# Block-diagonal gate products: one matmul of 512 tokens and one of 8 samples in place of two halves of 260

## The chip, the cores and the metric

The kernel runs on one core of a Trainium2 chip. The metric is the device time of one launch in microseconds; the median of three runs before the change is 1004.61 us (1003.96 to 1005.44). The core's engines are TensorE (PE in the profile, its weight loads PEld), VectorE (DVE), ScalarE (ACT), GpSimd (POOL) and SyncE (SP, which issues most transfers). Each has its own queue of instructions, in the order that the program gives it.

## The reference, cut to what matters

The kernel computes one inference step of a hybrid decoder layer for 512 prompt tokens and 8 samples of one token each, so 520 columns (tokens) of width 1024. The layer has two branches, a matrix recurrence (HGRN2, eight heads) and a vector recurrence (RG-LRU, eight blocks of 128 channels), then a merge, an output projection and an MLP. The change is in the RG-LRU gates:

```
def _blockdiag(x, w):
    B, L, _ = x.shape
    xb = x.reshape(B, L, LRU_BLOCKS, LRU_BS)
    return jnp.einsum('blnd,nde->blne', xb, w.astype(F32)).reshape(B, L, LRU_WIDTH)

xc, buf = _causal_conv(xb, st_conv[l], lru_conv_w[l], lru_conv_b[l])
r = jax.nn.sigmoid(_blockdiag(xc, lru_wa[l]) + lru_ba[l].astype(F32))
ig = jax.nn.sigmoid(_blockdiag(xc, lru_wx[l]) + lru_bx[l].astype(F32))
hseq, h_last = _rglru(xc, r, ig, lru_lambda[l], st_lru[l].astype(F32))
```

For each of the eight blocks there are two products of a 128 x 128 weight with 128 x 520 activations, each followed by a bias and a sigmoid.

## The kernel before

Channels lie on the 128 partitions and the 520 tokens along the free dimension. Every f32 operand of a large product is split into a high and a low part in the type f32r, and a product is three matmuls: high x high, high x low and low x high. The profile shows f32r as f32 in matmul rows.

The program has four parts: a start (loads, conditioning, first norm), the recurrences (eight heads in four pairs, with two RG-LRU blocks per pair), the gates, branch projections and output projection, and the MLP. During the recurrences the main stream on TensorE are the input projections (`gemm`, line 120): eight steps over the contraction, each three matmuls for each of two halves of 260 tokens. They write to `mm`, two tiles of two PSUM banks. Around them stand the heads' products: transposes (lines 592, 695, 737), the blocks of 32 (line 629), and the 128 x 128 products (lines 705, 718, 720).

An RG-LRU block n begins in `rg_x`: its two weights are loaded and split (line 765), its input comes from a projection, the convolution runs on VectorE and the result `xc` is split into `xcs` (line 185). Its gates are made one projection later, by `rg_gates`, called from `gemm`: `blockdiag` for r (weight `lru_wa`) and for the input gate (`lru_wx`). Before the change `blockdiag` takes the 520 tokens in two halves of 260. For each half it asks for a tile `pb`, multiplies three times (line 780) and takes the sigmoid on ScalarE (line 159) into a tile `gate` of 520 columns. Later the gates feed the scan (`rg_scans`).

PSUM has eight banks: `mm` four, `ppt` one (tile `pt`), `ppb` one (tile `pb`), and `pps` two (tile `ps`). `pps` is the small pool: the heads' blocks of 32 (line 629), the transposes of the values (lines 561 and 592) and the conditioning products use it in turn. A tile that is asked for while the banks are taken waits for the last reader of an earlier one.

The order on each engine is set by a scheduler that places instructions as their operands become ready in its own simulation of time; `behind` adds an order between two instructions without a wait, and `urgent` raises the priority of some. An instruction whose result is not ready holds up all that stand behind it on its engine.

Of the kernel before, what the change touches and what calls it, by code (L numbers as in the profile page):

```python
# [6 lines left out]
F32 = mybir.dt.float32  # L7
# [9 lines left out]
L = 512  # L17
NB = 8
T = L + NB
HALF = T // 2  # L20
# [31 lines left out]
class Kernel:  # L52
# [716 lines left out]
            r.append((hi, lo))  # L769
        return r  # L770

    def blockdiag(self, w, x, bias):
        nc = self.nc
        o = self.slot(self.hg, "gate")
        (wh, wl), (xh, xl) = w, x
        for s in range(2):
            c = slice(s * HALF, (s + 1) * HALF)
            ps = self.ppb.tile([128, 512], F32, name="pb")
            for n, (a, b) in enumerate(((wh, xh), (wh, xl), (wl, xh))):
                self.behind(nc.tensor.matmul(ps[:, :HALF], a, b[:, c], start=n == 0, stop=n == 2), self.last_product)  # L780
            self.sigmoid(o[:, c], ps[:, :HALF], bias=bias)
        return o

    def rg_x(self, n):
# [20 lines left out]
    def rg_gates(self):  # L805
        if self.rg_pending is None:
            return
        (n, w, xs, xc), self.rg_pending = self.rg_pending, None
        r = self.blockdiag(w[0], xs, self.ba[:, n:n + 1])
        g = self.blockdiag(w[1], xs, self.bx[:, n:n + 1])  # L810
        self.nc.vector.tensor_tensor(g, g, xc, OP.mult)
        self.rg[n] = r, g

# [965 lines left out]
```

## Time and profile before

| | |
|---|---|
| median of three runs | 1004.61 us |
| the profiled execution | 1004.8 us |
| its span from first to last instruction | 1003.0 us |
| TensorE busy | 981.2 us, 9585 matmuls |
| weight loads busy | 954.5 us, 9585 loads |
| VectorE busy | 694.2 us |
| ScalarE busy | 513.4 us |
| gate matmuls (line 780) | 96, first at 77.6 us, last at 370.9 us |
| gate sigmoids (`gate<-pb`) | 32, 479 ns each |

In a row of a group, the shape behind a matmul is active rows * active columns of the weight and then the moving operand; the numbers behind the bar are the busy time of the group in us, the mean duration of one in ns, and the idle time of its engine just ahead of it. Matmuls are pipelined, so their durations overlap; the distance from one start to the next, the step, is seen in a timeline, where rows of equal instructions are merged (start, length, count). A windows row shows the busy time of each engine in a stretch.

### The profile page before, as it was taken

To read this page: it belongs to the slowest core of one execution; us is meant where nothing else is said; L and a number is where in the kernel's file an instruction comes from. 1 tells how busy PE (TensorE), PEld (TensorE's weight loads), DVE (VectorE), ACT (ScalarE), POOL (GpSimd) and SP (SyncE) were. 2 spreads that over 40 slices of the span, in tenths; PEclk is the share of its full clock that TensorE was granted. 3 is DMA by queue.
4 is the path that set the end of the run, shared out by engine and by line. 5 is a ranking of instruction groups with operands and counts; after the bars stand their busy time and mean duration, and the time that the engine had idled before them with its cause. 6 is when DMAs were issued, how large, how long until landed. Compare 5 with 4: busy or idle time off the path is not lost.

```text
span 1003.0 us, 23261 instructions
## 1 busy us (share of the span) xinstructions
PE 981.2 (98%) x9585; PEld 954.5 (95%) x9585; DVE 694.2 (69%) x1546; ACT 513.4 (51%) x987; POOL 112.4 (11%) x194
## 2 busy tenths in 40 slices
PE   6999999999999999999999999999999999999996
PEld 4799999999999999999989999999999999999996
DVE  6789698697878867563332347767766776777686
ACT  5444844664584456351222234466556645646664
POOL 3000000000000000120000000012321331232151
PEclk9999999999999999999999999999999999999998
DMA  9885435344434434686567765222762483274242
GB/s 299 239 257 146 133 102 155 95 146 137 117 105 133 127 98 126 208 272 193 167 190 228 231 183 157 85 85 53 168 160 71 102 194 99 54 174 91 63 85 86
DMA packets 212572, 145.78 MB, mean 145 GB/s; under 512 B 6262, under 2 KB 196878, under 8 KB 212458
## 3 DMA queue, kind: packets, MB, share of 16 engines
q1 hardware_dynamic: 202562, 132.37, 44.5%
q0 software_dynamic: 9904, 11.92, 6.4%
q8 instruction: 75, 1.23, 0.5%
q14 instruction: 31, 0.25, 0.1%
HBM read 123.61 MB, written 13.39 MB: 137 GB/s over the span
## 4 chain that ended last, share of the span: by engine, by line
PE 93%; ACT 2%; SPq 2%; DVE 1%; DMA 1%; issue 1%; DVEq 0%; ACTq 0%
PE mm L120 67%; PE ps L1152 8%; PE pt L1152 4%; PE pb L1152 2%; PE ps L629 2%; PE ps L385 1%; PE pb L780 1%; DMA w<-in_w_in_dram 1%; SPq L374 1%; PE pt L705 1%; SPq L74 1%; PE pt L718 1%; PE pt L629 1%; PE pt L720 1%; PE ps L395 0%
## 5 line engine op out<-in xcount | busy, mean ns | idle before, releaser
L120 PE MATMUL mm<-h,whi 128*128 128x260 f32 x3040 | 502.8, 285 | 2.9 <-ACT h L481 1.9
L120 PEld LDWEIGHTS mm<-h,whi 128*128 128x128 f32 x3040 | 421.5, 189 | 8.4 <-ACT h L481 2.6
L120 PE MATMUL mm<-h,wlo 128*128 128x260 f32 x1520 | 310.8, 284 | 0.0
L85 ACT CAST whi<-wst 128x1024 fp32r<-128x1024 f32 x165 | 172.6, 1048 | 217.6 <-PE mm L120 178.7
L88 DVE TENSOR_TENSOR wlo<-wst,whi 128x1024 fp32r<-128x1024 f32 x165 | 201.2, 1220 | 89.6 <-ACT whi L85 88.2
L120 PEld LDWEIGHTS mm<-h,wlo 128*128 128x128 f32 x1520 | 237.0, 189 | 0.0
L120 PE MATMUL mm<-a,whi 128*128 128x260 f32 x512 | 82.8, 283 | 0.0
L120 PEld LDWEIGHTS mm<-a,whi 128*128 128x128 f32 x512 | 70.3, 188 | 0.9 <-issue 0.8
L120 PE MATMUL mm<-a,wlo 128*128 128x260 f32 x256 | 51.7, 284 | 0.0
L881 POOL DMA_DIRECT2D t<-oaT_d x8 | 4.3, 549 | 383.9 <-DMA oaT_d<-e 377.1
L1248 DVE TENSOR_TENSOR f<-f 128x260 f32<-128x260 f32 x64 | 27.3, 427 | 28.9 <-ACT f L1243 28.2
L1240 POOL TENSOR_TENSOR ft<-ft,fsh 128x8 f32<-128x8 f32 x28 | 18.4, 658 | 215.8 <-DVE ft L1234 215.8
L1237 ACT ACTIVATE ft<-ft,fsh 128x512 f32<-128x512 f32 (+2 forms) x36 | 24.1, 676 | 36.0 <-DVE ft L1234 36.0
L120 PE MATMUL mm<-b,whi 128*128 128x260 f32 x256 | 41.6, 284 | 0.0
L120 PEld LDWEIGHTS mm<-a,wlo 128*128 128x128 f32 x256 | 39.4, 188 | 0.0
L120 PEld LDWEIGHTS mm<-b,whi 128*128 128x128 f32 x256 | 35.0, 188 | 2.5 <-issue 2.5
L615 DVE TENSOR_TENSOR Y<-Y,tb 128x512 f32<-128x512 f32 x40 | 27.5, 687 | 9.1 <-PE ps L629 6.0
L1285 POOL DMA_DIRECT2D ma<-snap x28 | 26.8, 959 | 40.0 <-issue 22.1
L897 DVE TENSOR_TENSOR t<-mm,t 128x520 f32<-128x520 f32 x8 | 5.6, 699 | 37.0 <-PE mm L120 37.0
L1264 POOL DMA_DIRECT2D ma<-snap x28 | 26.6, 948 | 38.2 <-DMA ma<-snap 22.5
L1243 ACT ACTIVATE f<-ft 128x520 f32<-128x520 f32 (+1 forms) x36 | 20.7, 586 | 14.9 <-POOL ft L1241 12.9
L120 PE MATMUL mm<-b,wlo 128*128 128x260 f32 x128 | 25.8, 283 | 0.0
(489 smaller groups left out, 1839.2 us busy)
## 6 DMA issues: line engine op xcount, KB each, us to landing
wst<-in_w_in_dram SPq DMA_DIRECT2D x63, 512.0 KB
wm<-in_w_mod_dram SPq DMA_DIRECT2D x8, 2048.0 KB
wst<-in_w_ff_dram SPq DMA_DIRECT2D x32, 512.0 KB
wst<-in_w_ff_dram SPq DMA_DIRECT2D x64, 256.0 KB
wm<-in_w_mod_dram SPq DMA_DIRECT2D x8, 1024.0 KB
st<-in_state_hgrn_dram SPq DMA_DIRECT2D x8, 512.0 KB
vb<-vd SPq DMA_DIRECT2D x8, 512.0 KB
out_dram<-st SPq DMA_DIRECT2D x8, 512.0 KB
```

Source lines behind the costliest of these rows:

```text
L85: ins = self.nc.scalar.copy(hi, st)
L88: ins = self.nc.vector.tensor_tensor(lo, st, hi.bitcast(F32), OP.subtract)
L120: self.last_product = self.nc.tensor.matmul(out[:, :c.stop - c.start], x, y[:, c], start=first and n == 0, stop=last and n == 2)
L615: made = nc.vector.tensor_tensor(view(Y, b, 0, 2 * b, n, b), view(X, b, 0, 2 * b, n, b), fac, OP.mult)
L629: ins = nc.tensor.matmul(*args, start=True, stop=True)
L1152: ins = self.nc.tensor.matmul(ps, x[:, w], y[:, f], start=j in (1, 7, 2) and k == 0 and n == 0, stop=k == 3 and n == 2, skip_group_check=True)
L1237: nc.scalar.activation(t[:, :p], t[:, :p], AF.Relu, bias=sh[:, 0:1])
L1240: eng.tensor_tensor(t[:, p:], t[:, p:], sh[:, 1:9], OP.add)
L1243: nc.scalar.activation(f, self.two(self.ft)[:, a:a + n], AF.Square)
L1248: self.nc.vector.tensor_tensor(f[:, n], f[:, a], f[:, b], op)
L1264: nc.gpsimd.dma_start(x[1][:, b], v[:, :n], accum_op=OP.add)
L1285: nc.gpsimd.dma_start(x[t][:, a], s[p], accum_op=OP.add)
```

## The change

`blockdiag` no longer halves the tokens. It takes one tile `pb` for the 512 prompt tokens and a slice of 8 columns, `few`, for the samples. For each of the three products it issues one matmul of 512 columns into `pb` and one of 8 columns into `few`, both with the same weight. Two sigmoids follow, of 512 and of 8 columns. `rg_gates` asks for both `few` tiles in the small pool `pps` ahead of the two calls. The count of matmuls (96) and of sigmoids (32) is the same.

```
-    def blockdiag(self, w, x, bias):
-        nc = self.nc
+    def blockdiag(self, w, x, bias, few):
         o = self.slot(self.hg, "gate")
         (wh, wl), (xh, xl) = w, x
-        for s in range(2):
-            c = slice(s * HALF, (s + 1) * HALF)
-            ps = self.ppb.tile([128, 512], F32, name="pb")
-            for n, (a, b) in enumerate(((wh, xh), (wh, xl), (wl, xh))):
-                self.behind(nc.tensor.matmul(ps[:, :HALF], a, b[:, c], start=n == 0, stop=n == 2), self.last_product)
-            self.sigmoid(o[:, c], ps[:, :HALF], bias=bias)
+        ps = self.ppb.tile([128, 512], F32, name="pb")
+        for n, (a, b) in enumerate(((wh, xh), (wh, xl), (wl, xh))):
+            for out, c in ((ps, slice(0, L)), (few, slice(L, T))):
+                self.behind(self.nc.tensor.matmul(out, a, b[:, c], start=n == 0, stop=n == 2, skip_group_check=True), self.last_product)
+        self.sigmoid(o[:, :L], ps, bias=bias)
+        self.sigmoid(o[:, L:], few, bias=bias)
         return o
...
-        r = self.blockdiag(w[0], xs, self.ba[:, n:n + 1])
-        g = self.blockdiag(w[1], xs, self.bx[:, n:n + 1])
+        few = [self.pps.tile([128, 512], F32, name="ps")[:, :NB] for _ in range(2)]
+        r = self.blockdiag(w[0], xs, self.ba[:, n:n + 1], few[0])
+        g = self.blockdiag(w[1], xs, self.bx[:, n:n + 1], few[1])
```

The scheduler also places the work anew. The order changes on TensorE, ScalarE, VectorE and SyncE during the recurrences; on TensorE it is the same again behind the recurrences, and GpSimd's order does not change. Two places on TensorE show what moves.

The first is in the second pair of heads, block 2, where the gate matmuls stand among the projections (`mm<-h`) and the transposes of the keys (`pt<-ident,X`). The names `bdh` and `bdl` are the high and low part of a gate weight, `wa` of r and `wx` of the input gate. Before, from the second r matmul of the first half on:

```order
L120 MATMUL mm<-h,wlo 128x260 x2
L695 MATMUL pt<-ident,X 128x128 x3
L780 MATMUL pb<-xcs,bdhlru_wa 128x260
L780 MATMUL pb<-xcs,bdllru_wa 128x260
L695 MATMUL pt<-ident,X 128x128
L120 MATMUL mm<-h,whi 128x260 x4
```

The same place now:

```order
L120 MATMUL mm<-h,wlo 128x260
L695 MATMUL pt<-ident,X 128x128 x2
L778 MATMUL pb<-xcs,bdhlru_wa 128x512
L778 MATMUL ps<-xcs,bdhlru_wa 128x8
L778 MATMUL pb<-xcs,bdllru_wa 128x512
L778 MATMUL ps<-xcs,bdllru_wa 128x8
L695 MATMUL pt<-ident,X 128x128 x2
L120 MATMUL mm<-h,wlo 128x260
```

The r gate is done in one group of matmuls here, each of 512 columns followed by one of 8 with the same weight; the second half's group, some 25 matmuls later before, is gone.

The second place is block 3 of the same pair, on TensorE again. Before, at its first r matmuls (`pt<-g,X` is the end of a head's output product):

```order
L720 MATMUL pt<-g,X 128x128
L780 MATMUL pb<-xcs,bdhlru_wa 128x260
L120 MATMUL mm<-h,whi 128x260
L780 MATMUL pb<-xcs,bdhlru_wa 128x260
L780 MATMUL pb<-xcs,bdllru_wa 128x260
L120 MATMUL mm<-h,whi 128x260 x3
```

Now:

```order
L778 MATMUL ps<-xcs,bdhlru_wa 128x8
L778 MATMUL ps<-xcs,bdhlru_wx 128x8
L120 MATMUL mm<-h,whi 128x260 x2
L120 MATMUL mm<-h,wlo 128x260 x2
L120 MATMUL mm<-h,whi 128x260
L778 MATMUL pb<-xcs,bdhlru_wa 128x512 x2
L778 MATMUL ps<-xcs,bdhlru_wa 128x8
L778 MATMUL pb<-xcs,bdllru_wa 128x512
L778 MATMUL ps<-xcs,bdllru_wa 128x8
L778 MATMUL ps<-xcs,bdhlru_wx 128x8
L778 MATMUL ps<-xcs,bdllru_wx 128x8
L120 MATMUL mm<-h,whi 128x260 x3
```

The 8-column matmuls of both gates are taken ahead of or together with r's large ones, up to three in a row, since both `few` tiles are there from the start; the block's first gate matmul now stands ahead of the head's output products instead of behind them.

## The prediction

> **What bounds the kernel now.** I read the page's shares first, then the chain of waits, then TensorE in windows by stage.
>
> ```profile
> span 1003.0 us, 23261 instructions
> PE 981.2 (98%) x9585; PEld 954.5 (95%) x9585; DVE 694.2 (69%) x1546; ACT 513.4 (51%) x987; POOL 112.4 (11%) x194
> PE 93%; ACT 2%; SPq 2%; DVE 1%; DMA 1%; issue 1%; DVEq 0%; ACTq 0%
> ```
>
> TensorE is busy for 98% of the span and holds 93% of the chain that ended last. A share is a mean, so the stage with the gates decides. They run in four bursts, one per pair of heads. The windows by stage:
>
> ```profile
> core 0: us, PE busy (x) PEld busy (x) DVE busy (x) ACT busy (x) POOL busy (x), PEclk, DMA share, GB/s
> 58.00:100.00 42.00, 42.00 (x533) 41.62 (x532) 38.17 (x105) 20.78 (x49) 0.00 (x0) 1.00 0.69 199
> 100.00:140.00 40.00, 39.36 (x509) 38.78 (x508) 31.03 (x89) 26.57 (x50) 0.00 (x0) 1.00 0.42 125
> 140.00:260.00 120.00, 120.00 (x1548) 118.86 (x1548) 97.39 (x266) 66.06 (x149) 0.00 (x0) 1.00 0.45 129
> 260.00:385.00 125.00, 125.00 (x1591) 123.85 (x1590) 98.10 (x266) 73.97 (x160) 0.00 (x0) 1.00 0.40 116
> 385.00:680.00 295.00, 295.00 (x2450) 282.09 (x2450) 153.41 (x282) 111.34 (x170) 17.33 (x34) 1.00 0.58 177
> 680.00:990.00 310.00, 309.70 (x2556) 309.43 (x2555) 224.84 (x371) 181.21 (x345) 83.54 (x136) 1.00 0.45 106
> PE pt L705 <- ACT g L698: 0.6, 1, 0.6
> ```
>
> The last row is the whole list of TensorE's waits from 58 to 680 us: one, of 0.6 us. So from 58 us to 990 us TensorE is full at full clock, whatever it gains or loses in the gate stage reaches the end one for one, and a saving on any other engine buys at most that 0.6 us. The question is what a pair "512 columns and 8 columns" costs TensorE against a pair of 260s.
>
> **What is removed.** All gate products before, by line and shape:
>
> ```profile
> L780 PE MATMUL pb<-xcs,bdhlru_wa 128*128 128x260 f32 x32 | 8.7, 314 | 0.0
> L780 PE MATMUL pb<-xcs,bdhlru_wx 128*128 128x260 f32 x32 | 6.8, 293 | 0.0
> L780 PE MATMUL pb<-xcs,bdllru_wa 128*128 128x260 f32 x16 | 4.5, 283 | 0.0
> L780 PE MATMUL pb<-xcs,bdllru_wx 128*128 128x260 f32 x16 | 4.5, 282 | 0.0
> L780 PEld LDWEIGHTS pb<-xcs,bdhlru_wa 128*128 128x128 f32 x32 | 5.5, 189 | 0.2
> ```
>
> That is 96 matmuls, each with its own weight load even where the same weight follows twice. The duration (283 ns) is latency, not price, as matmuls overlap; the price is the step from start to start. From TensorE's timeline, with one group of three:
>
> ```profile
> 87.28 0.41 PE L780 MATMUL pb<-xcs,bdhlru_wa 128*128 128x260 f32 x2
> 87.52 0.28 PE L780 MATMUL pb<-xcs,bdllru_wa 128*128 128x260 f32 x1
> 87.64 0.28 PE L120 MATMUL mm<-h,wlo 128*128 128x260 f32 x1
> ```
>
> Three steps in 87.64 - 87.28 = 0.36 us, 120 ns each. Removed: 96 x 0.120 = 11.5 us; a pair costs 240 ns.
>
> **What is added: 48 matmuls of 512 columns.** The trace has none in this type (f32r, which its rows show as f32). Nearest rows:
>
> ```profile
> L629 PE MATMUL ps<-Y 128*32 128x32 f32 x1152 | 15.2, 198 | 0.0
> L629 PE MATMUL pt<-st,fkq 128*32 128x128 f32 x128 | 5.6, 276 | 0.0
> L385 PE MATMUL ps<-wm,cT 128*32 128x512 f32 x128 | 15.4, 598 | 0.0
> L120 PE MATMUL mm<-h,whi 128*128 128x260 f32 x2528 | 470.8, 285 | 2.9 <-ACT h L481 1.9 <-DVE h L484 0.9
> L120 PE MATMUL mm<-h,whi 128*128 128x270 f32 x512 | 136.4, 287 | 0.0
> ```
>
> The first three are plain f32: (598 - 276) / 384 = 0.84 ns per column on a fixed 276 - 128 x 0.84 = 169 ns. With that fixed part an f32r matmul takes (284 - 169) / 260 = 0.44 ns per column, so 512 columns step 120 + 252 x 0.44 = 231 ns. Bounds: if the whole 120 ns scales, 512 / 260 x 120 = 236; if only the 2 to 3 ns between the 260 and 270 rows count (0.3 per column), 196. I take 231: its slope stands on rows hundreds of columns apart, the lower bound on ten.
>
> **48 matmuls of 8 columns.** Their streaming is nothing (8 x 0.44 = 4 ns), but each brings a full 128 x 128 weight load. Nearest is the pair on line 750, 64 columns behind a full weight. The weight loads there, then the matmuls:
>
> ```profile
> 417.99 0.31 PEld L750 LDWEIGHTS ps<-sq,ones_r 128*128 128x128 f32 x2
> 418.21 0.19 PEld L120 LDWEIGHTS mm<-h,wlo 128*128 128x128 f32 x1
> 418.32 0.55 PEld L120 LDWEIGHTS mm<-h,whi 128*128 128x128 f32 x4
> 417.98 0.28 PE L120 MATMUL mm<-h,wlo 128*128 128x260 f32 x1
> 418.10 0.33 PE L750 MATMUL ps<-sq,ones_r 128*128 128x64 f32 x2
> ```
>
> 64 columns stream in 64 x 0.84 = 54 ns, yet the four loads start 417.99, two steps later 418.21, then 418.32: 110 ns apart. With little to stream, the load sets the step. The load behind an 8-column matmul can hide under only 4 ns of streaming, so that matmul costs 110 ns. The loader runs one matmul ahead: line 750's first load starts at 417.99, just when the matmul before it starts (417.98), and not under the one before that. Bounds: above, 120 (the step of a full 260); below, 7 to 13 ns (15.2 us / 1152 for the 32 x 32 blocks, which load 32 columns and overlap on separate quarters of the array). I take 110, because the width of the weight is that of line 750 and not of the blocks.
>
> The Trainium skill, page "TensorE: Matmul & The Clock Gate", section "Back-to-back issue gap", gives a matmul of 1 to 64 columns about 60 cycles (25 ns) and one of N columns N / 2.4 + 2.5 ns, as the isolated gap without a weight-load budget. By it a pair would go from 2 x 111 to 216 + 25 ns and the change would cost 48 x 19 ns = 0.9 us, an estimate from that page. The 110 ns of the 64-column pair above speak against its 25 ns here; the mechanism that would give it, a load already there, is the first rival, priced from rows.
>
> **Sum.** 48 x (231 + 110 - 240) ns = 48 x 101 = +4.8 us. With both lower ends 48 x (196 + 7 - 240) = -1.8; with both upper ends 48 x (236 + 120 - 240) = +5.6; with 196 and 110, +3.2. The order of the new program puts up to three 8-column matmuls behind each other; that changes nothing, each exposes one load.
>
> **ScalarE and the banks.** Rows for the sigmoids, and the longest part of the gates' own wait:
>
> ```profile
> L159 ACT ACTIVATE gate<-pb,pa 128x260 f32<-128x260 f32 x32 | 15.3, 479 | 16.1 <-PE pb L780 16.0
> L159 ACT ACTIVATE X<-mm 128x520 f32<-128x520 f32 x16 | 9.6, 600 | 0.0
> L1169 ACT ACTIVATE snap<-ps 128x8 f32<-128x8 f32 x14 | 2.4, 169 | 0.0
> ```
>
> A gate goes from 2 x 479 = 958 ns to about 600 + 169 = 769 ns: 16 x 0.19 = 3 us less on ScalarE, which waits 16 us for these very matmuls; worth 0. The cover of this zero is TensorE's full queue; without it 3 us would be the most.
>
> The bank of `pb` now has two users per block instead of four. Between them stand 24 to 27 projection matmuls, 3 us, against under 1 us for the sigmoid plus its queue. Both banks of `ps` go to the samples. The tight place is the second one, whose first 8-column matmul comes after the blocks of 32 of line 629, once their last reader is done. ScalarE and TensorE there, before the change:
>
> ```profile
> 166.31 1.16 PE L629 MATMUL ps<-Y 128*32 128x32 f32 x80
> 170.84 0.51 ACT L679 COPY at<-ps 32x128 f32<-32x128 f32 x2
> 171.37 0.48 ACT L159 ACTIVATE gate<-pb,pa 128x260 f32<-128x260 f32 x1
> ```
>
> The reader ends at 171.35, 3.9 us after 167.47. In the new order 51 matmuls stand between, some 6 us by 120 ns, so 2 us are left. Cost 0; between 0 and 1 us is kept for the range, like the 0.6 us above. If a matmul does wait there, all projection products behind it in TensorE's queue wait, and with them the casts of the next weights.
>
> The profiled execution took 1004.8 us (span 1003.0), 0.2 above the median of the runs, 1004.61. So 1004.8 + 4.8 = 1009.6, and 1009.4 for the median.
>
> **Rivals.** *A second load ahead.* In the 231 ns of a 512 there is time for two loads of 110. If the loader uses it, an 8-column matmul costs its 4 ns and the 5 ns by which 120 exceeds 260 x 0.44: the pair is 231 + 9 = 240, no change, 1004.6; with the 196 for the 512 even 1003, the other side. It decides at the first load behind an 8-column matmul: started under the 512 or not. Against it: line 750. The same skill page, section "What happens when you issue a matmul", says loads are pulled ahead into a background weight buffer, without saying how many; the loads quoted at 418 us show one.
>
> *The small banks.* The samples hold both `ps` banks, and a matmul waits for a reader of line 679 or a sigmoid that stands late in ScalarE's queue. It takes over when that reader comes 6 us after line 629; the casts of weights that stand in that queue take 1.05 us each, and three more of them ahead of the reader in each of four bursts would make 3.9 + 3.2 = 7.1 us, 1 us too late: +4.8 + 4 x 1, 1013.4. For it: the reader already lags 3.9 us. The casts:
>
> ```profile
> L85 ACT CAST whi<-wst 128x1024 fp32r<-128x1024 f32 x165 | 172.6, 1048 | 217.6 <-PE mm L120 178.7
> ```
>
>  Against it are the 2 us left.
>
> *Two passes.* Plain f32 products are recorded twice:
>
> ```profile
> L705 PE MATMUL pt<-g 128*128 128x128 f32 x64 | 8.5, 276 | 0.6 <-ACT g L698 0.6
> ```
>
> 64 records for 8 heads x 4. If so narrow an f32r product is run like that, 48 loads more: +5.3, 1014.7. Against: all f32r rows (line 780: 96 of 96) are single.
>
> **How the numbers follow.** Forecast 0.74 (1007.8 to 1010.6), second load ahead 0.10, small banks 0.10, two passes 0.04, something that gains 0.02. 0.2% (2 us) is about what this measurement can tell. Faster: 0.02 and 0.02 of the second-load case, 0.04; same 0.08; slower 0.88. The range reaches from 1007.0 (lower price of the 512, and a load 15 ns cheaper than 110) to 1011.8 (upper ends, 1.5 us of new waits).
>
> **What would show it.** Weight loads behind 8-column matmuls 110 ns apart and the step from an 8-column matmul to the next one near 110; 512-column steps of 225 to 236; TensorE still full from 58 to 680 us, with waits below 1 us; everything after 400 us shifted by 4 to 5 us and otherwise alike. Steps of 10 to 25 ns behind the 8 columns would make the forecast wrong, as would a TensorE wait on `ps` or `pb` in each burst.

## The result and the profile after

| | before | after |
|---|---|---|
| median of six runs | 1004.60 us | 1010.54 us |
| profiled execution | 1004.8 us | 1010.35 us |
| its span | 1003.0 us | 1008.6 us |

The ratio is 1.0060 (95% interval 1.0050 to 1.0071): slower by 5.9 us in the medians and 5.6 us between the two profiled executions. The forecast was 1009.4 us and the range 1007.0 to 1011.8. The page's shares and its chain of waits, after:

```profile
span 1008.6 us, 23270 instructions
PE 985.6 (98%) x9585; PEld 956.6 (95%) x9585; DVE 696.1 (69%) x1546; ACT 515.7 (51%) x987; POOL 112.8 (11%) x194
PE 89%; ACT 4%; DVE 3%; SPq 2%; DMA 1%; issue 1%; ACTq 0%; DVEq 0%
```

The count of matmuls is the same and TensorE is still 98% busy, but VectorE and ScalarE now hold 7% of the chain instead of 3%. TensorE's waits of the program from 58 us to 690 us are all in two rows; before, the only one was 0.6 us:

```profile
PE ps L629 <- DVE vs L563: 1.7, 4, 0.5
PE pt L737 <- ACT g L730: 0.2, 1, 0.2
```

That is 1.9 us against 0.6, or 1.3 us more. The rest is in the gate matmuls themselves. Block 3 in the last burst, first the matmuls, then the weight loads (start in us, length in us):

```profile
356.62 0.39 PE L778 MATMUL pb<-xcs,bdhlru_wa 128*128 128x512 f32 x1
356.85 0.17 PE L778 MATMUL ps<-xcs,bdhlru_wa 128*128 128x8 f32 x1
356.87 0.48 PE L778 MATMUL pb<-xcs,bdllru_wa 128*128 128x512 f32 x1
357.19 0.17 PE L778 MATMUL ps<-xcs,bdllru_wa 128*128 128x8 f32 x1
357.21 0.25 PE L778 MATMUL ps<-xcs,bdhlru_wx 128*128 128x8 f32 x1
```

```profile
356.62 0.19 PEld L778 LDWEIGHTS ps<-xcs,bdhlru_wa 128*128 128x128 f32 x1
356.85 0.19 PEld L778 LDWEIGHTS pb<-xcs,bdllru_wa 128*128 128x128 f32 x1
356.96 0.19 PEld L778 LDWEIGHTS ps<-xcs,bdllru_wa 128*128 128x128 f32 x1
357.19 0.19 PEld L778 LDWEIGHTS ps<-xcs,bdhlru_wx 128*128 128x128 f32 x1
357.30 0.19 PEld L778 LDWEIGHTS ps<-xcs,bdllru_wx 128*128 128x128 f32 x1
357.41 0.30 PEld L120 LDWEIGHTS mm<-h,wlo 128*128 128x128 f32 x2
```

The loads show the pace best. Each starts when the matmul before its own starts. Under a 512 the next load has 0.23 us (356.62 to 356.85, 356.96 to 357.19) and is hidden; behind an 8-column matmul the next one follows 0.11 us later (356.85 to 356.96, 357.19 to 357.30 to 357.41), with no columns to hide it. The recorded start of a matmul behind an 8-column one (356.87) is too early: it has 0.48 us of length instead of 0.39 and ends as if it had started with the next load, at 356.96. The steps below are therefore taken from the ends, less the usual length; which length is called usual (388 to 392 ns for a 512) moves a step by up to 4 ns.

All 48 small matmuls, by what follows them: another small one 18 times, 112 ns; a projection 16 times, 111; a 512 10 times, 107; a transpose of line 695, whose loads last 141 ns in the trace where a gate weight's last 188, 4 times, 63. Together 5.1 us. The 48 large ones step 231 to 236 ns, together 11.2 us. So 11.2 + 5.1 - 11.5 = +4.8 us. With the 1.3 us of waits that is 6.1. The span grew by 5.6, since the start, ahead of the change's place, went 0.6 us faster in this execution, as the first matmul of line 561 shows, before and after:

```profile
L561 PE MATMUL ps<-ident,e x8: 270/272/273, 63.3 to 369.8; 128*8 128x128 f32 x8
```

```profile
L561 PE MATMUL ps<-ident,e x8: 270/272/272, 62.7 to 375.2; 128*8 128x128 f32 x8
```

It is 0.6 us early at the first head (62.7 against 63.3) and 5.4 us late at the eighth. Behind the recurrences the two executions run in step, 5.5 us apart from the first conditioning product of line 385 to the end.

**Where the new waits come from.** TensorE waits for line 563 once in each of the four pairs of heads, for 0.4 to 0.5 us. Line 563 is VectorE's copy of the sample's values out of a `ps` bank. VectorE in the second head, before:

```profile
105.56 0.29 DVE L766 TENSOR_TENSOR bdllru_wa<-bdst,bdhlru_wa 128x128 fp32r<-128x128 f32 x1 [0.49 <-ACT bdhlru_wa L765]
106.97 0.28 DVE L563 COPY vs<-ps 8x128 f32<-8x128 f32 x1 [1.12 <-PE ps L561]
```

and after:

```profile
108.83 1.22 DVE L88 TENSOR_TENSOR wlo<-wst,whi 128x1024 fp32r<-128x1024 f32 x1
110.03 0.69 DVE L834 TENSOR_TENSOR gate<-gate,xc 128x520 f32<-128x520 f32 x1
110.78 1.22 DVE L836 TENSOR_TENSOR_SCAN hs<-ag,gate 128x512 f32<-128x512 f32 x1
112.11 0.28 DVE L563 COPY vs<-ps 8x128 f32<-8x128 f32 x1
```

Before, VectorE was idle and waited for line 561; after, the copy stands behind a scan and comes three microseconds after its matmul, while the blocks of line 629 wait for its bank. The scans stand there because the gates are done sooner. In this first pair ScalarE loads the tables for the scan's exponentials as soon as the last gate is done, before and after:

```profile
112.10 1.28 ACT L821 ACT_TABLE_LOAD   x1
```

```profile
98.09 0.69 ACT L159 ACTIVATE gate<-pb,pa 128x512 f32<-128x512 f32 x1
98.79 1.28 ACT L821 ACT_TABLE_LOAD   x1
```

The first pair's last gate is done 13 us earlier (10 to 14 us in the four pairs), and the scheduler places the scan's work ahead of the copy. In all seven variants below, each with two users of the one `pb` bank per block instead of four, that gate ends between 97.6 and 99.4 us (112.1 before), whatever the cut and with or without the small banks. That the number of users is what sets it was not tested by itself.

### The profile page after: what moved, and what is told of

Its sections match the earlier page's. It is cut to its first block, busy times and chain, and to the rows that moved or that the text cites. A ratio compares the mean times of both kernels' runs of the same rounds, so it can differ in the third digit from the quotient of the medians.

```text
span 1008.6 us, 23270 instructions
## 1 busy us (share of the span) xinstructions
PE 985.6 (98%) x9585; PEld 956.6 (95%) x9585; DVE 696.1 (69%) x1546; ACT 515.7 (51%) x987; POOL 112.8 (11%) x194
## 4 chain that ended last, share of the span: by engine, by line
PE 89%; ACT 4%; DVE 3%; SPq 2%; DMA 1%; issue 1%; ACTq 0%; DVEq 0%
PE mm L120 64%; PE ps L1152 8%; PE pt L1152 4%; PE pb L1152 2%; PE ps L629 2%; PE ps L385 1%; PE pb L778 1%; DMA w<-in_w_in_dram 1%; SPq L374 1%; PE pt L629 1%; PE pt L705 1%; SPq L74 1%; DVE wlo L88 1%; ACT ag L821 1%; DVE gate L834 1%
```

## The experiments

Two theories were set against each other. *Load*: an 8-column matmul costs the weight load that its columns cannot hide. *Order*: the 8 columns are cheap, and the time lies in waits that the new banks and the new order bring. In the table the ratio is to the kernel before, on the same chip; the waits are TensorE's in the recurrences, from each run's trace.

| run | median us | ratio (95%) | waits us |
|---|---|---|---|
| the change | 1010.54 | 1.0060 (1.0050 to 1.0071) | 1.9 |
| 8 columns twice | 1017.19 | 1.0122 (1.0105 to 1.0139) | 1.2 |
| no 8 columns | 1006.24 | 1.0014 (1.0004 to 1.0023) | 2.2 |
| operands swapped | 1009.02 | 1.0040 (1.0025 to 1.0055) | 1.4 |
| scans later | 1009.24 | 1.0044 (1.0027 to 1.0060) | 0.8 |
| old cut, new banks | 1006.12 | 1.0017 (1.0008 to 1.0026) | 1.8 |
| cut at 392 | 1008.15 | 1.0044 (1.0027 to 1.0061) | 2.1 |
| old cut, scans later | 1004.75 | 1.0002 (0.9992 to 1.0013) | 0.7 |

**The 8 columns twice.**

```
-            for out, c in ((ps, slice(0, L)), (few, slice(L, T))):
+            for out, c in ((ps, slice(0, L)), (few, slice(L, T)), (few, slice(L, T))):
```

> The change, with each matmul of 8 columns issued twice in a row (48 more). The samples' gates are wrong by it: products are counted twice. Load theory (a matmul of 8 columns costs the 110 ns of the weight load that its 4 ns of columns cannot hide): 48 x 0.110 = +5.3 us over the changed kernel's 1010.5, 1015.8, and steps of 110 to 112 ns from one 8-column matmul to the next. Order theory (the 8 columns are cheap, the 5.9 us come from new waits in the new order): within 1 us of 1010.5.

The small corrections are counted twice here, the large product once, since its first matmul starts the sum anew. It took 1017.19 us, and the profiled execution 1015.46. The weight loads of one group, which follow each other:

```profile
355.26 0.53 PEld L778 LDWEIGHTS ps<-xcs,bdhlru_wx 128*128 128x128 f32 x4
355.71 0.30 PEld L778 LDWEIGHTS ps<-xcs,bdllru_wx 128*128 128x128 f32 x2
355.93 0.30 PEld L778 LDWEIGHTS pb<-xcs,bdhlru_wx 128*128 128x128 f32 x2
```

Six steps from load to load make 355.26 to 355.93, 112 ns each. 48 more matmuls brought 5.1 us in the profiled executions (1010.35 to 1015.46), in which the waits fell by 0.7, and 6.6 in the medians, whose four runs spread over 4 us. 48 x 0.112 = 5.4 us is the load's part; what the medians have beyond it is not explained. The order theory's "within 1 us" falls.

**No 8 columns.** The small matmuls and their banks are gone.

```
-            for out, c in ((ps, slice(0, L)), (few, slice(L, T))):
-                self.behind(self.nc.tensor.matmul(out, a, b[:, c], start=n == 0, stop=n == 2, skip_group_check=True), self.last_product)
+            self.behind(self.nc.tensor.matmul(ps, a, b[:, :L], start=n == 0, stop=n == 2, skip_group_check=True), self.last_product)
...
-        self.sigmoid(o[:, L:], few, bias=bias)
+        self.sigmoid(o[:, L:], ps[:, :NB], bias=bias)
...
```

> The change without the matmuls of 8 columns and without their banks; the samples' gates are left out (their sigmoid reads 8 columns of the prompt's instead). Load theory: 48 x 0.110 = 5.3 us less than 1010.5, 1005.2, with the 512-column steps still near 235 ns. Order theory: the waits stay, so above 1008.

1006.24 us, 4.3 less than the change instead of 5.3, and 1.3 above the kernel before that ran beside it (1004.99) although it does less. The order theory's "above 1008" falls too. The 512s step 231 ns here. TensorE's waits:

```profile
PE ps L629 <- DVE hlast L837: 1.1, 3, 0.5
PE pt L695 <- ACT sev L683: 0.6, 1, 0.6
PE pt L583 <- DVE e L738: 0.5, 1, 0.5
```

2.2 us, 1.6 more than before. The 512s save 96 x 0.120 - 48 x 0.231 = 0.4 us, so 1.6 - 0.4 = 1.2 us, and 1.3 was measured. So the small matmuls are most of the change's price, and waits of this size come with the earlier gates even where the small pool is left alone: they do not need the small banks.

**Operands swapped.** The 8 sample columns become the weight and the gate weight streams.

```
...
+            self.behind(self.nc.tensor.matmul(few, b[:, L:T], a, start=n == 0, stop=n == 2, skip_group_check=True), self.last_product)
...
-        self.sigmoid(o[:, L:], few, bias=bias)
+        self.sigmoid(o[:, L:], ps[:, :NB], bias=bias)
+        self.nc.scalar.copy(self.sm.tile([NB, 8], F32, name="gt", bufs=1), few[:, :8])
...
```

A copy on ScalarE reads the small tile in place of the small sigmoid, which takes 8 of the prompt's columns.

> The change with the operands of the small matmul swapped: the 8 sample columns are the weight (a load 8 wide) and the 128 x 128 gate weight streams as 128 columns. The samples' gates are left out, as the small product comes out turned. Load theory: the small matmul now costs its columns, 128 x 0.44 = 57 ns instead of 110, so 48 x 0.053 = 2.5 us less, 1008.0. If any small matmul had a fixed price of 110 ns whatever its weight: 1010.5.

1009.02 us: 1.5 less, not 2.5. The expectation took the wrong load. The loads in its last burst:

```profile
355.97 0.19 PEld L777 LDWEIGHTS pb<-xcs,bdllru_wa 128*128 128x128 f32 x1
356.08 0.09 PEld L778 LDWEIGHTS ps<-bdllru_wa,xcs 128*8 128x8 f32 x1
356.32 0.09 PEld L778 LDWEIGHTS ps<-bdhlru_wx,xcs 128*8 128x8 f32 x1
356.38 0.09 PEld L778 LDWEIGHTS ps<-bdllru_wx,xcs 128*8 128x8 f32 x1
356.44 0.42 PEld L120 LDWEIGHTS mm<-h,whi 128*128 128x128 f32 x3
```

Between two small matmuls the pace is now 60 ns (356.32, 356.38, 356.44), in place of 112, because the load in between is 8 wide. Ahead of a full weight it is still 110 (355.97 to 356.08), although 128 columns stream meanwhile. So the price of a short matmul is the load of the matmul *behind* it, where that is longer than its own columns. By ends, the 17 small ones with another small one behind them gained 52 ns each, 0.9 us; waits fell by 0.5.

**Cut at 392.**

```
-            for out, c in ((ps, slice(0, L)), (few, slice(L, T))):
+            for out, c in ((ps[:, :392], slice(0, 392)), (few, slice(392, T))):
...
```

The two sigmoids follow the same cut.

> The same with the cut at 392 and 128 columns. The 392 step by the measured 0.46 ns per column is 180 ns. Load theory: the 128 columns stream in 57 ns, less than a load, so they cost 110 as the 8 do: the pair 290 ns, 48 x 0.055 = 2.6 us less than 1010.5, 1007.9. If a small matmul costs its columns and a hand-over of 5 ns: 180 + 62 = 242, 1005.6.

1008.15 us, where the load theory said 1007.9 and the other 1005.6. The input gate in one block, whose 392s and 128s stand together:

```profile
87.04 0.52 PE L778 MATMUL pb<-xcs,bdhlru_wx 128*128 128x392 f32 x2
87.40 0.34 PE L778 MATMUL pb<-xcs,bdllru_wx 128*128 128x392 f32 x1
87.58 0.34 PE L778 MATMUL ps<-xcs,bdhlru_wx 128*128 128x128 f32 x2
87.75 0.27 PE L778 MATMUL ps<-xcs,bdllru_wx 128*128 128x128 f32 x1
```

The three 392s take 0.54 us, 180 ns each. The 128s, by ends, step 108 to 112 ns, the same as the 8s with a sixteenth of the columns. The load sets both.

**Old cut, new banks.** The first 260 columns go to `pb`, the other 260 to `ps`.

```
-            for out, c in ((ps, slice(0, L)), (few, slice(L, T))):
+            for out, c in ((ps[:, :HALF], slice(0, HALF)), (few, slice(HALF, T))):
...
```

The two sigmoids take a half each.

> The change's banks and order, with the old cut: one matmul of the first 260 columns into the large tile and one of the other 260 into the small pool's. Load theory: the pair costs 240 ns again, so 48 x (235 + 110 - 240) ns = 5.0 us less than 1010.5, 1005.5, with the 1 to 2 us of waits behind the scans still there. Bank theory (the samples' use of the small pool costs the time): stays within 1 us of 1010.5.

1006.12 us: 4.4 less than the change. The gate steps are 120 ns again (117 ahead of a transpose). It stays 1.8 us above the kernel before that ran beside it (0.8 to 2.6 by the interval), and 1.2 of that is in the waits, 1.8 us against 0.6:

```profile
PE ps L629 <- DVE vs L563: 0.9, 2, 0.5
PE ps L629 <- DVE hlast L839: 0.6, 2, 0.4
PE pt L737 <- ACT g L730: 0.3, 2, 0.2
```

**Scans later.** VectorE's part of the scans is placed behind the copy of line 563.

```
-            nc.vector.tensor_tensor(g, g, u, OP.mult)
...
+            self.behind(nc.vector.tensor_tensor(g, g, u, OP.mult), self.vs_copied)
...
```

The loop that begins here moves into a function of its own, which each second head calls behind that copy.

> The change, with VectorE's part of the scans placed behind the copy of the sample's values (line 563). TensorE waited 1.7 us in four pieces for that copy in the changed kernel and not at all before. Order theory for this part: the waits of line 629 on line 563 go, 1.3 us less net, 1009.2, and the other 5 us stay. If those waits only stand in for a later one: 1010.5.

1009.24 us, 1.3 less, as expected. The waits on line 563 (565 in this kernel) are gone, and one of another kind is left:

```profile
PE pt L585 <- DVE hlast L845: 0.8, 1, 0.8
```

The two intervals of the totals overlap (1.0027 to 1.0060 and 1.0050 to 1.0071), so the totals alone do not tell the two apart; it is the waits in the trace that show it.

**Old cut and scans later**, both of these edits together.

> Both undone: the old cut of 260 and 260 in the change's banks, and the scans behind the copy of line 563. If the load (5.0 us) and the waits behind the scans (1 to 1.5 us) are the whole of the loss, it takes the time of the kernel before, 1004.6 within 0.7 us, and TensorE waits less than 0.9 us from 58 us to the end of the recurrences. If the small pool has a price of its own, it stays at 1006 as the old cut alone.

1004.75 us against 1004.72 for the kernel before that ran beside it (ratio 1.0002, 0.9992 to 1.0013), with the samples' banks in the small pool:

```profile
PE pt L697 <- ACT sev L685: 0.7, 1, 0.7
```

The gates end as early here as in the change (97.6 us in the first pair), so it is the place of the scans, and not the early gates by themselves, that makes TensorE wait. With the cut and the scans undone nothing of the loss is left that this measurement can tell, and the small pool has no price that it shows; the interval leaves room for 1.3 us at most. No run beats the kernel before: its 260s hide every load (120 ns each, 0.46 per column), and the 512's 231 to 236 ns are the same 0.45 to 0.46 per column, so a longer matmul has nothing to save.

## Why the prediction was right

- *TensorE is the bound and passes on what it loses.* Right: behind the recurrences all stands 5.5 us later (forecast: 4 to 5) and is otherwise alike.
- *A 512 steps 231 ns.* Right: 231 to 236. The choice between 231 and the 236 of plain scaling, which rested on a fixed part borrowed from plain f32 rows, is not decided by this; over 48 matmuls it is 0.2 us.
- *An 8-column matmul costs 110 ns.* Right in size: 107 to 112, and 63 where a transpose follows. The forecast gave the reason loosely. It said that the load "behind an 8-column matmul" cannot hide, which holds, and beside it that "each brings a full 128 x 128 weight load", as if the price were its own. The swapped run tells the two apart: it is the next matmul's load.
- *Sum +4.8 us.* Right by its steps: 11.2 + 5.1 - 11.5 = 4.8.
- *New waits cost 0.* This term was too small. It measured 1.3 us (1.9 against 0.6), beyond the 0 to 1 us that this step kept and within the 1.5 us that the range's upper end held. It is about all of the 1.1 us by which the forecast of 1009.4 fell short. The place was wrong too: the second `ps` bank and the reader of line 679 did not hold TensorE up. The step looked at the gates' own banks alone. The gates ended 13 us earlier, the scans moved ahead of line 563 on VectorE, and the blocks of line 629 waited for that copy. "Worth 0" for an engine with time to spare was right as a gain and missed that work that becomes ready earlier takes another place in the queue.
- *The signs.* Two of the signs went against the forecast: waits "below 1 us" became 1.9, and a TensorE wait on `ps` came in each burst, which was to make the forecast wrong. It held even so, because each of these waits is 0.4 to 0.5 us and not the 1 us of that rival: a sign of this kind needs a size.
- *ScalarE's 769 ns per gate.* Too low, and without effect. The sigmoids, after:

```profile
L159 ACT ACTIVATE gate<-pb,pa x16: 682/689/696, 84.4 to 361.3; 128x512 f32<-128x512 f32 x16
L159 ACT ACTIVATE gate<-ps,pa x16: 256/262/270, 84.9 to 358.1; 128x8 f32<-128x8 f32 x16
```

689 + 262 = 951 ns against 958. The rows taken as nearest were sigmoids and copies without a bias operand; the old gate, at 479 ns for 260 columns, would have been nearer.

- *Rivals.* A second load ahead: no; the loads start one matmul ahead in every row above. The small banks: the waits are on `ps`, but behind line 563 and 0.3 us a burst net, not 1 us behind line 679. Two passes: no, 48 records for 48 small matmuls.

## What to carry to other kernels

On a full TensorE, price a matmul as the longer of its own columns and the next matmul's weight load; here columns run at 0.46 ns and a full f32r load takes 110, so a part of fewer than some 240 columns (110 / 0.46, an estimate) with a full load behind it costs that load whatever its width, as the 8 and the 128 did, and a cut with both parts above that, as 260 and 260, costs no more per column than a 512. When a change makes a side product ready earlier under a scheduler that places by readiness, look at which work its later steps now stand ahead of on the other engines. A kernel made of both parts undone, and found equal to the one before, closes such an account better than the parts alone.

## What the runs showed of the hardware that was not expected

- The load that a short matmul exposes is that of its successor: 60 ns ahead of an 8-wide load, some 110 ahead of a 128-wide one, for the same short matmul of 128 columns.
- The profile's recorded start of a matmul behind an 8-column one is some 85 ns too early (0.48 us of length for a 512 that takes 0.39 elsewhere); weight-load starts and matmul ends give the steps.
- A sigmoid of 8 columns with a bias out of PSUM took 262 ns where a scaled copy of the same shape takes 169 (`snap`, line 1169).
